# First block of a two-block network on one core: scores in two 128-row passes, value products in two rounded passes, gate projections ahead of the attention

## The chip, the cores and the metric

The kernel runs on one core of a Trainium2 chip. TensorE (PE) multiplies, with its weight loads shown as PEld; VectorE (DVE), ScalarE (ACT) and GpSimd (POOL) work on what it leaves; SyncE (SP) issues the transfers. The metric is the device time of one execution in microseconds (us), lower is better. The change is compared by the median of several runs.

## The reference, cut to what matters

The network has two blocks over 512 tokens of width 1024. The change touches the first block alone, a hybrid attention layer, everything in float32:

```python
qn = rope(rms_norm(heads(q_n)));  o_cmp, p = compressed_branch(qn, kc_cmp, vc_cmp)   # 31 compressed keys
o_sel = selected_branch(qn, ks, vs, sel_idx);  o_win = window_branch(qn, kw, vw)      # 512 keys, causal
o_nsa = (g0 * o_cmp + g1 * o_sel + g2 * o_win) * silu(z_n)
o_dsa = dsa_branch(qd, kd, vd, qi, ki, wi) * silu(z_d)       # each query keeps its 128 best keys
x = x + concat([o_nsa, o_dsa]) @ w_out
```

There are two groups (g) of four query heads (r) each, 64 channels a head, for each of two query sets (s = 0: the three branches of o_nsa, s = 1: o_dsa). The second block (two layers of feed-forward, mixing and feed-forward) follows and is not touched.

## The kernel before

Float32 accuracy is kept by splitting: `split` (L255 to L257) writes a rounded part hi with a copy on ACT and the remainder lo with a subtraction, on DVE by default. Rounded operands (F32R) take one pass of TensorE for each product, plain float32 ones are shown as two matmul records. `wload` (L259 to L264) loads 512 KB of weights and splits them (names raw, whi, wlo); `proj` (L501) is one projection of 128 columns: 24 matmuls of 512 columns into a bank "B", for the eight k-tiles of the input times the three products of hi and lo.

Block 1 is `block1` (L401). It emits, in this order: the projections 0 to 7 (indexer, compressed keys and values, keys) with the token-major values `tok` among them; the query projections 8 to 15, whose outputs are rotated (`rope`, L470) and stacked by `stack_q` and `stack_k` (L486 to L495); then the gate projections 16 and 17 (`post_z`, L783). `drain` (called at L833) then emits what is left of the background tasks, among them `topk` (L600), the choice of the 128 best keys: 16 rounds of MAX8 and MATCH_REPLACE8 on DVE for each of the query tiles 3, 2 and 1. Before that, `topk` is emitted at one round per 4.5 us of nominal product time.

The attention follows. Query tiles of 128 are taken in the order i = 3, 2, 1, 0, with keys up to n = 128 (i + 1). Each i has six steps (`step`, L839): for s = 0 two branches in each of two groups, for s = 1 one in each of two groups. A step makes four score tiles (one a head) in banks "A", takes them through a masked minimum on DVE (L852) and an exponential on ACT (L855), scales the rows by the reciprocal of their sum (DVE, ACT and POOL, L859 to L869), transposes each block of 128 keys (L878) into a bank "C", copies it to PT (L881 on ACT, L883 on DVE) and multiplies it with the values into a bank "D". A score takes two passes (`stacked`, L497): 128 rows hold the query's hi and lo against the key's hi twice, then 64 rows hold the query's hi against the key's lo. The value product is a plain float32 product with 64 output rows; both groups share one bank. `compressed` (L936) does the same for the compressed keys. `finish` (L925) multiplies the result by the gate z and splits it. The gate projections 18 to 23 are emitted one after each of the first six steps (`extra`, L1011; `more`, L1016), the first half of the output projections (`wout`, L989) after i = 2.

Emission order is a priority. A scheduler orders each engine's instructions: an instruction that is ready may go ahead of one emitted before it that is not. Memory is handed on tile by tile: a pool opened where another was closed waits for that one's last readers. The pool of the attention (PA) is opened where the projections' pool (PX) was.

Of the kernel before, what the change touches and what calls it, by code (L numbers as in the profile page):

```python
# [16 lines left out]
EPS = 1e-6  # L17
# [7 lines left out]
# ---------------------------------------------------------------- constants of the shapes  # L25
def _constants():
# [46 lines left out]
    # window over number of tokens in it, first and last eight tokens  # L73
# [10 lines left out]
    # rows p of the Fourier matrices; columns by residue of the frequency, 0 2 1 3 mod 4 and 0 1 mod 2  # L84
# [8 lines left out]
# ---------------------------------------------------------------- layout of the inputs  # L93
# [93 lines left out]
# columns of the packed per-partition vectors  # L187
# [13 lines left out]
class Tensor:  # L201
    """the tensor engine, with its newest product at hand"""
# [13 lines left out]
def build(tc, I, out, taps=None):  # L216
# [37 lines left out]
    # ------------------------------------------------------------ helpers  # L254
# [37 lines left out]
    def colsum(ps, sqs, nt):  # L292
        """ps[:, i] = sums over the partitions of the tiles in sqs, tokens on the partitions"""
# [5 lines left out]
    def rowcast(ps, cols, nt):  # L299
        """ps[p, t] = cols[t] on every partition"""  # L300
# [4 lines left out]
    # ------------------------------------------------------------ adaptive modulation  # L305
# [34 lines left out]
    def ada_done(l, c0, c1):  # L340
        """chunks c0..c1 of the nine become usable"""
# [13 lines left out]
    def wait(t):  # L355
        """the steps of a thread until t microseconds of products have been emitted"""
# [9 lines left out]
    def pace(t):  # L366
        """run a step of each background task per `every` microseconds of products"""
# [32 lines left out]
    # ------------------------------------------------------------ block 1  # L400
    def block1(fill, lh):  # L401
# [3 lines left out]
        XS = mkpool("xs", stack=b1)  # L405
        p1, pj = ExitStack(), ExitStack()
        P1 = mkpool("b1", stack=p1)
        PX = mkpool("pj", stack=pj)
# [8 lines left out]
        def bank(tag):  # L417
            return tl(PS, [128, 512], F32, tag, {"A": 3, "B": 2, "C": 2, "D": 1}[tag])
# [7 lines left out]
        def load_x():  # L426
# [5 lines left out]
            for k in range(KT):  # L432
                hi = tl(XS, [128, L], F32R, f"xhi{k}")
                lo = tl(XS, [128, L], F32R, f"xlo{k}")
# [30 lines left out]
            rb = tl(XS, [128, L], F32, "rb")  # L465
# [49 lines left out]
        # indexer queries and keys  # L515
# [17 lines left out]
        # token-major: values, gates, indexer weights  # L533
# [1486 lines left out]
```

## Time and profile before

| | |
|---|---|
| median of 3 runs | 3105.65 us |
| the runs | 3103.13, 3109.27, 3105.65 us |
| profiled execution | span 3109.3 us |
| PE, DVE, ACT, POOL busy share of the span | 97%, 57%, 44%, 33% |

The span agrees to the rounding with the highest of the three times, so nothing is seen to lie outside it. The PE share is an upper view: ends of matmuls are modelled, so the spacing of their starts says more than their durations. Views by stretch (busy time in each part of the span) tell which engine is full in which stage, the chain tells what the end waited for, and the groups give the duration of one instruction of a shape.

### The profile page before, as it was taken

The page shows a single profiled execution, that of the slowest core. Times are in us where ns is not written, and L with a number is a line of the kernel's source. Part 1 is how long each engine was busy: PE and PEld are TensorE (multiplying, and loading weights), DVE is VectorE, ACT ScalarE, POOL GpSimd, SP SyncE. Part 2 cuts the span into 40 slices and gives each one's busy share as a digit, 9 for nine tenths or more (in the row PEclk, how much of TensorE's full clock was granted, in tenths as well). Part 3 has the DMA queues.
Part 4 walks back from the last instruction along what each step waited for, and adds up shares of the span by engine and source line. Part 5 has one row for each costly group of instructions (what it writes and reads, how often), then busy time and mean ns, then how long its engine had stood idle before and what let it go on. Part 6 is the DMA issues. An engine that isn't in the chain of part 4 may idle for free.

```text
span 3109.3 us, 42513 instructions
## 1 busy us (share of the span) xinstructions
PE 3016.6 (97%) x16956; PEld 2521.5 (81%) x16956; DVE 1763.0 (57%) x3104; ACT 1363.7 (44%) x2410; POOL 1035.1 (33%) x556
## 2 busy tenths in 40 slices
PE   7799999999999999999999999999999999999998
PEld 6565467888888887678888888888888887698998
DVE  6996546764646536566667445443433457554545
ACT  6545546545535434445555344321322345442324
POOL 6763122667666222026896421000000142200001
PEclk9899899999999999999999999999999999999999
DMA  5311013333333311023444432121122221123223
GB/s 203 130 55 48 1 41 105 127 129 129 122 135 115 94 43 53 21 68 130 149 146 160 162 109 67 63 67 62 61 62 68 67 81 65 36 95 95 90 94 94
DMA packets 81720, 282.85 MB, mean 91 GB/s; under 512 B 9328, under 2 KB 13040, under 8 KB 80880
## 3 DMA queue, kind: packets, MB, share of 16 engines
q1 hardware_dynamic: 81520, 280.13, 27.3%
q8 instruction: 133, 2.18, 0.3%
q14 instruction: 67, 0.55, 0.1%
HBM read 277.99 MB, written 2.10 MB: 90 GB/s over the span
## 4 chain that ended last, share of the span: by engine, by line
PE 82%; DVE 9%; POOL 3%; ACT 3%; issue 2%; DMA 1%; SPq 0%; DVEq 0%; POOLq 0%; ACTq 0%
PE ps L209 72%; PE B L209 3%; PE A L209 3%; PE D L209 2%; POOL ajunk L332 2%; DVE wlo L257 1%; PE C L878 1%; POOL araw L332 1%; DMA araw<-in_ada_dram 1%; PE ps L1825 1%; DVE dm L606 1%; ACT whi L256 1%; DVE xll L1136 1%; DVE nt L1159 1%; DVE m L605 1%
## 5 line engine op out<-in xcount | busy, mean ns | idle before, releaser
L256 ACT ACTIVATE whi<-raw 128x1024 fp32r<-128x1024 f32 (+2 forms) x370 | 382.7, 1035 | 983.1 <-PE ps L209 764.4
L209 PE MATMUL ps<-xhl,whi 128*128 128x512 f32 (+2 forms) x1856 | 638.4, 352 | 3.1 <-ACT whi L256 1.6
L209 PE MATMUL ps<-xll,whi 128*128 128x512 f32 (+2 forms) x1856 | 635.9, 351 | 0.0
L209 PE MATMUL ps<-xhl,wlo 128*128 128x512 f32 (+2 forms) x1856 | 596.4, 351 | 6.3 <-DVE wlo L257 6.3
L257 DVE TENSOR_TENSOR wlo<-raw,whi 128x1024 fp32r<-128x1024 f32 (+2 forms) x342 | 501.3, 1467 | 127.5 <-ACT whi L256 120.3
L332 POOL TENSOR_TENSOR araw<-araw,cc 128x1024 f32<-128x1024 f32 x144 | 408.7, 2839 | 94.4 <-DMA araw<-in_ada_dram 80.0
L209 PEld LDWEIGHTS ps<-xhl,whi 128*128 128x128 f32 x1856 | 351.0, 189 | 51.3 <-ACT whi L256 2.0
L332 POOL TENSOR_TENSOR ajunk<-araw,cc 128x1024 f32<-128x1024 f32 x112 | 290.1, 2590 | 255.2 <-DMA araw<-in_ada_dram 234.9
L209 PEld LDWEIGHTS ps<-xll,whi 128*128 128x128 f32 x1856 | 352.3, 190 | 3.8
L209 PEld LDWEIGHTS ps<-xhl,wlo 128*128 128x128 f32 x1856 | 328.1, 190 | 11.4 <-DVE wlo L257 7.5
L209 PE MATMUL ps<-xlc,whi 128*128 128x258 f32 (+1 forms) x1112 | 315.6, 284 | 1.5 <-DVE xlc L1168 0.8
L209 PE MATMUL ps<-xhc,wlo 128*128 128x258 f32 (+1 forms) x1112 | 312.9, 282 | 0.0
L209 PE MATMUL ps<-xhc,whi 128*128 128x258 f32 (+1 forms) x1112 | 312.3, 282 | 0.4 <-ACT xhc L1167 0.4
L1096 POOL TENSOR_TENSOR accl<-accl,nt 128x512 f32<-128x512 f32 x24 | 33.4, 1390 | 800.1 <-ACT nt L1092 799.7
L209 PE MATMUL ps<-hll,whi 128*128 128x512 f32 (+1 forms) x752 | 284.8, 379 | 0.7 <-DVE hll L257 0.7
L209 PE MATMUL ps<-hhl,wlo 128*128 128x512 f32 (+1 forms) x752 | 285.3, 380 | 0.0
L209 PE MATMUL ps<-hhl,whi 128*128 128x512 f32 (+1 forms) x752 | 283.9, 379 | 0.0
L1271 DVE SCALAR_TENSOR_TENSOR hl<-ps,gtl,hl 128x512 f32<-128x512 f32 (+1 forms) x104 | 73.0, 709 | 350.7 <-PE ps L209 350.5
L209 PEld LDWEIGHTS ps<-xlc,whi 128*128 128x128 f32 x1112 | 209.4, 188 | 48.7 <-DVE xlc L1168 1.8
L209 PEld LDWEIGHTS ps<-xhc,whi 128*128 128x128 f32 x1112 | 208.8, 188 | 48.3 <-PE ps L209 1.7
L209 PEld LDWEIGHTS ps<-xhc,wlo 128*128 128x128 f32 x1112 | 210.5, 189 | 0.0
L1204 DVE SCALAR_TENSOR_TENSOR ps<-ps,rbl 128x512 f32<-128x512 f32 (+1 forms) x110 | 63.0, 590 | 236.6 <-PE ps L209 236.6
(578 smaller groups left out, 5905.4 us busy)
## 6 DMA issues: line engine op xcount, KB each, us to landing
raw<-in_w_dram SPq DMA_DIRECT2D x240, 512.0 KB, 3.5
araw<-in_ada_dram SPq DMA_DIRECT2D x144, 512.0 KB, 4.3
raw<-in_wo_dram SPq DMA_DIRECT2D x36, 512.0 KB, 3.4
raw<-in_wi_dram SPq DMA_DIRECT2D x34, 512.0 KB, 3.4
raw<-in_w_dram SPq DMA_DIRECT2D x36, 384.0 KB, 3.1
raw<-in_wg_dram SPq DMA_DIRECT2D x8, 512.0 KB, 3.5
cc<-in_cc_dram SPq DMA_DIRECT2D x3, 1024.0 KB, 5.0
sm<-in_sm_dram SPq DMA_DIRECT2D x2, 1282.0 KB, 7.1
```

What stands on the lines that cost most here:

```text
L209: self.newest = self.engine.matmul(*a, **k)
L256: S.activation(hi, x, AF.Copy)
L257: eng.tensor_tensor(out=lo, in0=x, in1=hi.bitcast(F32), op=ALU.subtract)
L332: m = G.tensor_tensor(out=o, in0=raw, in1=cc[:, v], op=ALU.mult)
L605: V.max(out=m8, in_=wk)
L606: V.match_replace(out=wk, in_to_replace=m8, in_values=wk, imm_value=-2e30)
L878: T.transpose(pt[:, 128 * r:128 * r + 128], Pm[:, r, 128 * kt:128 * kt + 128], ident)
L1096: (V if i == 7 else G).tensor_tensor(out=st.acc[:, c], in0=st.acc[:, c], in1=sq, op=ALU.add)
L1136: V.scalar_tensor_tensor(out=lo, in0=h, scalar=a, in1=hi.bitcast(F32), op0=ALU.mult, op1=ALU.subtract)
L1159: V.scalar_tensor_tensor(out=t, in0=st.h[k][:, c], scalar=st.A[:, k:k + 1], in1=st.rb[:, c], op0=ALU.mult, op1=ALU.mult)
L1204: V.scalar_tensor_tensor(out=pb, in0=pb, scalar=0.5, in1=rb, op0=ALU.mult, op1=ALU.mult)
L1271: V.scalar_tensor_tensor(out=st.h[m][:, c], in0=a, scalar=gates[st.name][:, m:m + 1], in1=st.h[m][:, c], op0=ALU.mult, op1=ALU.add)
```

## The change

Scores: the key's lo part is also written twice, so the second pass has 128 rows too. Values: hi and lo of the values lie beside each other as 128 stationary columns, the transposed probabilities are split into hi and lo, and two F32R passes replace the float32 product; each group has its own bank, and `gather` adds the two halves of it. All eight gate projections come before the attention, the input's second half is released then, and the forced emission of `topk` at that place is gone. Banks: A 3 to 2, D 1 to 2.

```diff
-            return tl(PS, [128, 512], F32, tag, {"A": 3, "B": 2, "C": 2, "D": 1}[tag])
+            return tl(PS, [128, 512], F32, tag, {"A": 2, "B": 2, "C": 2, "D": 2}[tag])
...
-                V.tensor_tensor(out=k[2][GS[g]], in0=y[GS[g]], in1=k[g][GS[g]].bitcast(F32), op=ALU.subtract)
+                V.tensor_tensor(out=k[2 + g][GS[g]], in0=y[GS[g]], in1=k[g][GS[g]].bitcast(F32), op=ALU.subtract)
                 S.activation(k[g][GS[1 - g]], y[GS[g]], AF.Copy)
+                S.activation(k[2 + g][GS[1 - g]], k[2 + g][GS[g]].bitcast(F32), AF.Copy)
...
             T.matmul(ps, q[g][:, qs], k[g][:, :n], start=True, stop=False)
-            T.matmul(ps, q[g][GS[g], qs], k[2][GS[g], :n], start=False, stop=True)
+            T.matmul(ps, q[g][:, qs], k[2 + g][:, :n], start=False, stop=True)
...
-                    S.activation(vt[i], pst[i][:, 0:384], AF.Copy, scale=rc[:, i:i + 1])
+                    pv_ = pst[i][:, 0:384].rearrange("p (b g d) -> p b g d", b=3, g=2)
+                    for g in range(2):
+                        hi, lo = vt[i][:, :, g, g], vt[i][:, :, g, 1 - g]
+                        S.activation(hi, pv_[:, :, g], AF.Copy, scale=rc[:, i:i + 1])
+                        V.scalar_tensor_tensor(out=lo, in0=pv_[:, :, g], scalar=rc[:, i:i + 1], in1=hi.bitcast(F32),
+                                               op0=ALU.mult, op1=ALU.subtract)
...
-        proj(16, post_z(0, 0))
-        proj(17, post_z(0, 1))
+        flush()
+        for b in list(bg):
+            if b[0] is fill:
+                for _ in fill:
+                    pass
+                bg.remove(b)
+        aes.close()
+        PZ = mkpool("pz", stack=p1, side="right")
+        zz.extend(tl(PZ, [128, 4, L], F32, f"z{n_}") for n_ in range(2))
+        for n_ in range(2):
+            for r in range(4):
+                proj(16 + 4 * n_ + r, post_z(n_, r), G if r % 2 else V)
         flush()
         while threads:
             advance()
         pj.close()
-
-        # attention
+        xe.close()
         at = ExitStack()
-        drain()
-        aes.close()
         PA = mkpool("at", stack=at)
-        zz.append(tl(PA, [128, 4, L], F32, "z1"))
...
-                    PT = PTs[kt] = tl(PA, [128, L], F32, "PT", 3)
-                    if kt % 2 == 0 or i == 3:
-                        S.activation(PT, pt, AF.Copy)
-                    else:
-                        V.tensor_copy(PT, pt)
+                    PTs[kt] = [tl(PA, [128, L], F32R, f"PT{p}", 3) for p in "hl"]
+                    split(*PTs[kt], pt)
...
-                        state["acc"] = bank("D")
-                    acc = state["acc"]
-                    T.matmul(acc[gs, :], vt[kt][:, vcol + 64 * g:vcol + 64 * g + 64], PTs[kt],
-                             start=gcol is None and kt == 0, stop=last and kt == i)
-                    if fin and kt == i:
-                        finish(acc, i, s)
+                        state["acc", g] = bank("D")
+                    acc = state["acc", g]
+                    v = vt[kt][:, br, g].rearrange("p a d -> p (a d)")
+                    for n_, P_ in enumerate(PTs[kt]):
+                        T.matmul(acc, v, P_, start=first and kt == n_ == 0, stop=last and kt == i and n_ == 1)
+                    if last and kt == i:
+                        gather(acc, i, s, g)
...
+        def gather(acc, i, s, g):
+            if g == 0:
+                state["o"] = tl(PA, [128, 4, 128], F32, "o", 2)
+            o = state["o"]
+            og = o[GS[g]].rearrange("p r q -> p (r q)")
+            S.activation(og, acc[GS[1 - g]], AF.Copy)
+            V.tensor_tensor(out=og, in0=acc[GS[g]], in1=og, op=ALU.add)
+            if g == 0:
+                return
...
-            V.scalar_tensor_tensor(out=o, in0=acc.rearrange("p (r q) -> p r q", r=4), scalar=0.5,
-                                   in1=zz[s][:, :, sl], op0=ALU.mult, op1=ALU.mult)
+            V.tensor_tensor(out=o, in0=o, in1=zz[s][:, :, sl], op=ALU.mult)
...
-        extra = [lambda r=r: proj(16 + r, post_z(0, r), G) for r in (2, 3)]
-        extra += [lambda r=r: proj(20 + r, post_z(1, r), G) for r in range(4)]
+        extra = []
```

The compressed branch gets the same split of its probabilities and values; `post_z` folds the factor 0.5 in.

## Rows read from the trace of the kernel before

**Rows 1.** Busy time by stretch: each engine's us (instructions), granted clock, DMA.
```profile
130.00:245.00 115.00, 97.68 (x422) 76.12 (x420) 111.52 (x228) 55.22 (x81) 72.00 (x43) 0.90 0.20 69
...
245.00:489.00 244.00, 241.24 (x962) 137.39 (x962) 124.23 (x377) 122.40 (x310) 52.57 (x33) 0.92 0.11 35
```

**Rows 2.** The chain that ended last, 245 to 489 us, shares by line.
```profile
by line: PE A L209 28.8%; PE D L209 28.5%; PE B L209 24.6%; PE C L878 15.0%; PE C L970 1.7%; DVE o L929 0.6%; ACT PT L881 0.2%; ACT xhi L256 0.2%; DVE dm L606 0.2%; DVE P L852 0.1%; issue 0.1%; DVE Pc L947 0.1%; DVE den L859 0.0%; DVE mx L8
```

**Rows 3.** DVE in order of time (start, us): first score and last gating.
```profile
245.38 0.73 DVE L852 CUSTOM_DVE_ANT_0 P<-A,blk1c,rq0y 128x512 f32<-128x512 f32 x1
...
488.16 0.69 DVE L929 SCALAR_TENSOR_TENSOR o<-D,z 128x512 f32<-128x512 f32 x1 [4.26 <-PE D L209]
```

**Rows 4.** PE in order of time, 276 to 289 us (start, us, xcount).
```profile
276.82 0.40 PE L209 MATMUL B<-xhi,whi 128*128 128x512 f32 x1
277.05 0.39 PE L209 MATMUL B<-xlo,whi 128*128 128x512 f32 x1
...
283.33 2.60 PE L209 MATMUL A<-k,q 128*128 128x512 f32 x6
285.86 0.50 PE L209 MATMUL B<-xhi,whi 128*128 128x512 f32 x1
...
287.69 1.07 PE L209 MATMUL D<-PT,v 128*64 128x512 f32 x2
288.70 0.66 PE L878 MATMUL C<-cst,P 128*128 128x128 f32 x4
```

**Rows 5.** PE groups by shape, 245 to 489 us: xcount, busy, mean ns, idle before.
```profile
L209 PE MATMUL D<-PT,v 128*64 128x512 f32 x120 | 67.5, 650 | 1.5 <-DVE den L859 0.9 <-ACT PT L881 0.6
L878 PE MATMUL C<-cst,P 128*128 128x128 f32 x240 | 42.0, 299 | 0.0
...
L209 PE MATMUL B<-xhi,wlo 128*128 128x512 f32 x34 | 14.4, 424 | 0.0
```

**Rows 6.** DVE groups by shape, 245 to 489 us.
```profile
L883 DVE COPY PT<-C 128x512 f32<-128x512 f32 x12 | 8.3, 690 | 13.9 <-PE C L878 12.1 <-PE D L209 1.7
...
L789 DVE SCALAR_TENSOR_TENSOR z<-zt,z 128x512 f32<-128x512 f32 x6 | 7.8, 1304 | 2.1 <-ACT zt L788 2.1
...
L859 DVE RECIPROCAL den<-den 128x4 f32<-128x4 f32 x24 | 4.2, 174 | 10.2 <-ACT P L855 10.2
L786 DVE TENSOR_TENSOR z<-B,rb 128x512 f32<-128x512 f32 x6 | 4.1, 687 | 7.3 <-PE B L209 7.3
```

**Rows 7.** ACT groups by shape, 245 to 489 us.
```profile
L881 ACT ACTIVATE PT<-C 128x512 f32<-128x512 f32 x48 | 28.4, 595 | 59.0 <-PE C L878 58.8
...
L256 ACT ACTIVATE whi<-raw 128x1024 fp32r<-128x1024 f32 x13 | 13.7, 1051 | 13.5 <-PE B L209 7.3 <-issue 6.2
...
L788 ACT ACTIVATE zt<-z 128x512 f32<-128x512 f32 x6 | 3.7, 621 | 0.0
```

**Rows 8.** The choice of keys on DVE: groups, 120 to 250 us.
```profile
L605 DVE MAX8 m<-dm 128x8 f32<-128x384 f32 x16 | 8.8, 552 | 0.2
L606 DVE MATCH_REPLACE8 dm<-m,dm 128x384 f32<-128x384 f32 x16 | 8.7, 542 | 0.1
...
L605 DVE MAX8 m<-dm 128x8 f32<-128x256 f32 x16 | 6.8, 423 | 0.2
L606 DVE MATCH_REPLACE8 dm<-m,dm 128x256 f32<-128x256 f32 x16 | 6.5, 409 | 0.1
```

**Rows 9.** The same in order of time: its first round and its last operation.
```profile
123.92 0.69 DVE L605 MAX8 m<-dm 128x8 f32<-128x512 f32 x1
...
246.04 0.28 DVE L608 TENSOR_SCALAR dm<-dm 128x256 f32<-128x256 f32 x1
```

**Rows 10.** Busy time by stretch where PE has gaps; columns as in rows 1.
```profile
130.00:140.00 10.00, 4.57 (x26) 3.71 (x24) 10.00 (x16) 5.44 (x9) 5.96 (x3) 0.84 0.49 171
140.00:150.00 10.00, 6.25 (x29) 5.79 (x30) 8.95 (x14) 2.30 (x4) 6.72 (x4) 0.65 0.39 148
150.00:160.00 10.00, 10.00 (x47) 7.42 (x45) 9.04 (x17) 3.14 (x5) 9.33 (x6) 1.00 0.16 53
```

More of the change, by code (lines that the diff above doesn't have):

```diff
@@ L432, in load_x @@
             for k in range(KT):
-                hi = tl(XS, [128, L], F32R, f"xhi{k}")
-                lo = tl(XS, [128, L], F32R, f"xlo{k}")
+                hi, lo = (tl(XA if k < 4 else XB, [128, L], F32R, f"x{p}{k}") for p in ("hi", "lo"))
                 g = vec[:, V_NG + k:V_NG + k + 1]
@@ L531, in post_ki @@
             rope(y, ki)
-        vt = [tl(P1, [128, 384], F32, f"v{i}") for i in range(4)]
+        vt = [tl(P1, [128, 3, 2, 2, 64], F32R, f"v{i}") for i in range(4)]
         gate = tl(P1, [128, 4, 24], F32, "gate")
@@ L609, in topk, with qtile @@
                 chosen[0] = i
-        kT = [[tl(P1, [128, L], F32R, f"k{n}{a}") for a in range(3)] for n in range(3)]
-        qT = [[tl(P1, [128, L], F32R, f"q{n}{a}") for a in range(2)] for n in range(8)]
-        kcT = [tl(P1, [128, 32], F32R, f"kc{n}") for n in range(3)]
-        vc = tl(P1, [31, 2, 64], F32, "vc")
+        kT = [[tl(P1, [128, L], F32R, f"k{n}{a}") for a in range(4)] for n in range(3)]
+        qT = [None] * 8
+        def qtile(n, a, dt=F32R):
+            return tl(P1, [128, L], dt, f"q{n}{a}")
+        kcT = [tl(P1, [128, 32], F32R, f"kc{n}") for n in range(4)]
+        vc = tl(P1, [31, 2, 2, 64], F32R, "vc")
         parts = {}
@@ L631, in post @@
                                     op=ALU.add)
-                    hi, lo = (q[:, 0:496] for q in qT[4 + 2 * ci + half])
+                    hi, lo = (qtile(4 + 2 * ci + half, n_)[:, 0:496] for n_ in range(2))
                     split(hi, lo, a.rearrange("p g c r -> p (g c r)"))
@@ L684, in ctail @@
                                  cw2[:, 256 + 64 * m:320 + 64 * m], start=m == 0, stop=m == 1)
-                V.tensor_copy(vc.rearrange("p g d -> p (g d)"), po[0:31, 0:128])
+                for g in range(2):
+                    split(vc[:, g, g], vc[:, g, 1 - g], po[0:31, 64 * g:64 * g + 64])
                 return
@@ L713, in block1 @@
         kms = tl(PX, [128, 3, 4, 2], F32, "kms")
-        zz = [tl(P1, [128, 4, L], F32, "z0")]
-        ky = [zz[0][:, n] for n in range(3)]
+        ky = [qtile(2 + n // 2, n % 2, F32) for n in range(3)]
         def post_k(n_, gcol):
@@ L830, in block1, with step @@
         pj.close()
+        xe.close()
         at = ExitStack()
-        drain()
-        aes.close()
         PA = mkpool("at", stack=at)
-        zz.append(tl(PA, [128, 4, L], F32, "z1"))
         state = {}
-        def step(i, g, s, kTt, mask, vcol, gcol, first, last, fin, ahead=[], behind=[]):
+        def step(i, g, s, kTt, mask, br, gcol, first, last, fin, ahead=[], behind=[]):
             n = 128 * (i + 1)
-            gs = slice(64 * g, 64 * g + 64)
             q4, rq4 = qT[4 * s:4 * s + 4], rq[s]
@@ L977, in f @@
                 def f():
-                    if g == 0:
-                        state["acc"] = bank("D")
-                    T.matmul(state["acc"][64 * g:64 * g + 64, :], vc[:, g], PTs[g], start=True, stop=False)
+                    acc = state["acc", g] = bank("D")
+                    v = vc[:, g].rearrange("p a d -> p (a d)")
+                    for n_, P_ in enumerate(PTs[g]):
+                        T.matmul(acc, v, P_, start=n_ == 0, stop=False)
                 return f
@@ L1022, in block1 @@
             if i % 2:
-                pool, th, tlo = (PA, "ohi", "olo") if i == 3 else (XS, "xhi", "xlo")
-                state["oh", i // 2] = [(tl(pool, [128, 2, 256], F32R, f"{th}{a}"),
-                                        tl(pool, [128, 2, 256], F32R, f"{tlo}{a}")) for a in range(4)]
+                pool, tag = (PA, "o") if i == 3 else (XA, "x")
+                state["oh", i // 2] = [[tl(pool, [128, 2, 256], F32R, f"{tag}{p}{a}") for p in ("hi", "lo")]
+                                       for a in range(4)]
             n = 128 * (i + 1)
@@ L1033, in block1 @@
                 more(i)
[L1034 removed]
+                step(i, g, 0, kT[1], mask, 1, 2, False, True, g == 1)
                 more(i)
```

33 lines of the change are left out of this document (16 added, 17 removed).

## The prediction, made before the changed kernel was run

> **What bounds the kernel now.** I read the view by stretch first, since the share over the whole span (PE 97%) mixes stages. In the last stretch ahead of the attention, 130 to 245 us, DVE is busy 111.5 of 115 us and PE 97.7 [rows 1]: the choice of keys, the rotations and the splits fill DVE, and PE waits for it now and then. From 245 to 489 us, the attention, it is the other way round: PE 241.2 of 244 us, DVE 124.2, ACT 122.4 [rows 1]. The chain of the same stretch agrees: 98% of it is PE, and by banks the scores (A) take 28.8%, the value products (D) 28.5%, the gate projections and output projections (B) 24.6%, the transposes (C) 15% [rows 2]. The attention runs from its first score on DVE at 245.4 to the end of the last gating at 488.9 us: 243.5 us [rows 3]. So the change works on the engine that binds here, and the question is what binds once PE is relieved.
>
> **The change part by part.** Only starts tell what a matmul costs, so prices are spacings.
>
> Scores. Dense projections of 512 columns start 0.23 us apart. A run of six score matmuls, 128 rows and 64 rows in turn, takes from 283.33 to 285.86 us, 0.42 each [rows 4]. The 24 steps have 4 heads and 2 passes, 192 such matmuls. If two passes of 128 rows go at the dense spacing, each saves 0.19 us; I take the same for the narrower tiles, and nothing for the compressed branch: 192 x 0.19 = 36 us of PE. The bounds are 0 (the spacing has another cause) and about 40. The Trainium skill says in "TensorE: Matmul & The Clock Gate", section "Why this matters for your kernels", that a single product with few rows takes the same time as one with 128. By that rule this part would save nothing on PE. The six score matmuls speak against it [rows 4], though they don't say whether the row count or the alternation costs the 0.19; it is a rival below.
>
> Value products. One is two records and takes 287.69 to 288.70 us, 1.0 us [rows 4]; there are 60 of them (120 records, [rows 5]) and 8 in the compressed branch. Two F32R passes at 0.23 take 0.46: 68 x 0.54 = 37 us of PE saved.
>
> Gates. 100 matmuls of gate projections lie behind 245 us (34 in the group shown and 33 in each of the two others, [rows 5]). There they fill time in which PE would wait for the softmax. Moved ahead they cost 100 x 0.23 = 23 us, and the attention's tiles lie in memory that the projections' temporaries and part of the input held, so its first softmax waits for the last gate's evacuation too: 0.69 + 0.62 + 1.30 = 2.6 us [rows 6, 7]. The attention starts 25.6 us later. Nothing hides this: that stage had PE busy 85%, but its gaps come from waits on DVE that the gates, being emitted last, meet only at the end. From below, one projection (5.5 us) and the 2.6 us may be hidden: 17.5; from above 28. The move also changes which engine splits two of the gates' weights (POOL to DVE) and where their eight 512 KB loads stand in SP's queue: each has the 5.5 us of a projection, and DMA is 20% busy there [rows 1].
>
> PE's sum in the attention is then 241 - 23 - 36 - 37 = 145 us.
>
> DVE. It loses the six gates' evacuations (4.1 + 7.8 us) and 12 copies to PT (8.3 us) [rows 6]. It gains the lo part of every transposed block, 68 subtractions out of PSUM; the nearest row is the copy out of PSUM of the same size, 0.69 us [rows 6]: 47 us. It gains 16 half additions in gather at the same price, 11 us. 124.2 - 11.9 - 8.3 + 47 + 11 = 162 us.
>
> ACT. It loses six weight copies (6.3) and six tanh (3.7), and gains 12 copies to PT and 16 in gather at about 0.6 [rows 7]: 122.4 - 10 + 17 = 129 us.
>
> So DVE becomes the bound of the attention, with ACT close behind, and each now waits for the other twice a step: DVE for the exponential's sums, ACT for the scores, and new, DVE's subtraction for ACT's hi copy. The 162 us can't be reached. DVE waited 10.2 us for the exponentials ahead of the reciprocals [rows 6], and that stays: 172 is the lower end. The upper end adds one whole hi copy, 0.595 us [rows 7], to each of the 68 subtractions: 172 + 40 = 212. Neither row is nearer (DVE always has other heads' scores to take, but only two banks A now, and its order is fixed), so I take the middle, 192 us. Two banks A instead of three lie within these ends: a score waits until DVE has taken the one two before it, and behind it on PE wait the transposes that ACT needs.
>
> Choice of keys. Emitted at one round per 4.5 us, eight queries, one compressed unit and eight gates (8 x 5.1 + 1.3 + 8 x 5.1 = 83 us) bring 18 of 48 rounds ahead of the attention, and the forced rest is gone. But before, only 11 rounds were emitted ahead of the forced ones, and yet the rounds ran steadily from 123.9 to 246 us [rows 9], beside the query projections. A ready round is taken forward whenever DVE is free in the plan, so I expect them there again and cost the move at nothing; the cover is the 25 us by which the stage grows. If it is gone, 30 rounds, 14 x (0.55 + 0.54) + 16 x (0.42 + 0.41) = 29 us of DVE [rows 8], land in the attention.
>
> Values and keys. The values' evacuation has four more copies on ACT, some 2 us at most, 0 at least: 1 us taken. The keys' extra eight copies on ACT lie beside a DVE that is fuller (ACT 55 of 115 us, [rows 1]): nothing. The second block is the same.
>
> Sum against the profiled execution: 3109.3 + 25.6 - (243.5 - 192) + 1 = 3084.4 us. The median lies 3.65 below the profiled execution: 3080.8, so 3081 us. With 172 and 17.5 it is 3053, with 212 and 28 3103.
>
> **The rivals.**
>
> Rival 1, PE still binds or DVE loses nothing to waits. For it: PE fills 99% of the stage today [rows 1], and the order is planned with all waits known. Attention 162 us, start 17.5 later: 3043 us. Against it: the lo parts wait for ACT by construction.
>
> Rival 2, the choice of keys moves into the attention. DVE has 162 + 29 there, with 10 to 50 us of waits 201 to 241, middle 221; the stage before gets back up to half of PE's 17 us of gaps [rows 1], 8 us: 3105.65 + 25.6 - 8 - 22.5 + 1 = 3102 us, no change that can be told.
>
> Rival 3, on the other side: the granted clock falls. With the gates gone PE has 145 us of work in 192, 75% busy. Where PE had gaps, 46% and 63% busy at 130 to 150 us, the clock was 0.84 and 0.65, and back at 1.00 in the next 10 us with PE full [rows 10]; in the attention it is 0.92 [rows 1], so the 145 us are 133 at full speed. If a share x of the work ran at 1.2 GHz, PE would need 133 (1 + x). It passes DVE's 192 at x = 0.44 and makes the kernel slower beyond 218 us, x = 0.64. At x = 0.8 it is 240: 3105.65 + 25.6 - 3.5 + 1 = 3129 us. Against it: even 130 to 150 us had only half at the low level. The Trainium skill ("TensorE: Matmul & The Clock Gate", section "PE-mode transpose") says that transposes don't count as activity for the clock as products do; the attention keeps its 240 transposes [rows 5] and loses products, so by that rule this rival gains. No row here separates the two.
>
> Rival 4, the change doesn't do what it says: two 128-row passes also start 0.42 apart. PE has 145 + 36 = 181 us, still under 192 but no longer hidden: some 205 us, 3094 us.
>
> **How the numbers follow.** Forecast 0.56 (3053 to 3103), rival 1 0.11 (3043), rival 2 0.13 (3102), rival 3 0.14 (3129), rival 4 0.06 (3094). About 0.2% (6 us) is what can be told from no change. Faster: nearly all of the forecast (0.51), rivals 1 and 4 (0.16), a little of rival 2: 0.70. Same: 0.14. Slower: 0.16. The range leaves out most of rival 1 below and rival 3 above: 3050 to 3110 us.
>
> **What would show it.** By stretch, the attention's first score near 271 us, DVE the fullest engine behind it, PE near 75%. Score matmuls 0.23 apart, value products 0.46. DVE's subtractions out of PSUM 0.69 us each, idle ahead of them put down to ACT's hi copy. MAX8 over by about 270 us. The prediction is wrong if the score spacing stays 0.42, if MAX8 is seen among the scores, if the clock in the attention falls under 0.7, or if the attention starts before 260 or takes over 215 us.

## The result, and the profile after

The changed kernel takes 3068.9 us (3064.84 to 3069.45), the kernel before beside it 3105.8 us: a ratio of 0.9878, 95% interval 0.986 to 0.9895. It is 1.2% faster. The prediction said 3081 us, with a range from 3050 to 3110: the direction and the range held, and the gain is 12 us larger than forecast. The profiled execution has a span of 3067.5 us, 41.8 us less than that of before, though the medians lie only 36.9 us apart: a span is some 1.8 us shorter than its execution's time (3067.5 against 3069.37 here), so the 3109.3 us profiled before belong, by that estimate, to an execution of some 3111 us, slower than the three runs listed with it; that the span met the highest of them was chance.

Busy time by stretch, the kernel after (columns as in [rows 1]: stretch, length, then PE, PEld, DVE, ACT and POOL in us, granted clock, DMA):

```profile
130.00:245.00 115.00, 100.57 (x424) 77.46 (x424) 109.69 (x235) 57.52 (x89) 70.56 (x42) 0.88 0.21 69
245.00:275.00 30.00, 24.53 (x108) 19.85 (x109) 19.04 (x23) 9.82 (x12) 9.52 (x4) 0.96 0.28 90
275.00:447.00 172.00, 155.31 (x864) 119.23 (x863) 153.96 (x433) 128.72 (x328) 42.19 (x28) 0.93 0.10 34
447.00:3067.00 2620.00, 2572.01 (x15108) 2223.50 (x15108) 1438.47 (x2389) 1105.84 (x1884) 818.07 (x440) 0.99 0.29 93
```

The stretch 130 to 245 us is nearly what it was. A new one follows, 30 us of gate projections. The attention has shrunk, and taken as a whole no engine fills it: PE 155, DVE 154 and ACT 129 of 172 us, where PE had 241 of 244 [rows 1]. That is a mean over four query tiles with different limits; the tiles i = 3, 2, 1 and 0 end near 335, 375, 422 and 447 us:

```profile
275.00:335.00 60.00, 54.49 (x255) 35.98 (x254) 56.68 (x141) 46.54 (x108) 12.02 (x7) 0.94 0.02 8
335.00:375.00 40.00, 36.53 (x205) 26.80 (x205) 37.43 (x110) 32.08 (x83) 8.52 (x6) 1.00 0.01 1
375.00:422.00 47.00, 44.29 (x322) 39.17 (x320) 42.34 (x116) 34.26 (x86) 19.85 (x12) 1.00 0.28 91
422.00:447.00 25.00, 20.00 (x86) 17.28 (x85) 17.51 (x70) 15.83 (x53) 1.81 (x3) 0.65 0.13 42
```

DVE is busy 94% of the first two, PE 94% of the third, which also holds output projections, and no engine fills the last, where the granted clock is 0.65.

The edges of the attention, DVE in order of time (start, us, then the instruction, in brackets the idle time ahead of it):

```profile
271.48 2.41 DVE L802 SCALAR_TENSOR_TENSOR z<-t,z 128x512 f32<-128x512 f32 x1 [0.73 <-ACT t L801]
273.81 0.47 DVE L972 TENSOR_TENSOR Pc<-A,blk1c 128x124 f32<-128x124 f32 x2
...
275.47 0.75 DVE L872 CUSTOM_DVE_ANT_0 P<-A,blk1c,rq0y 128x512 f32<-128x512 f32 x1 [0.29 <-PE A L209]
...
445.77 0.69 DVE L955 TENSOR_TENSOR o<-o,z 128x512 f32<-128x512 f32 x1
```

From the first score at 275.47 to the end of the last gating at 446.46 it is 171.0 us, against 243.5 [rows 3]. In the terms of the prediction's sum:

| us | forecast | measured |
| --- | --- | --- |
| first score later (gates, values) | +25.6 +1 | +30.1 |
| attention | -51.5 | -72.5 |
| what lies behind it (2620.4 before, 2621.0 after) | 0 | +0.6 |
| sum | -24.9 | -41.8 |

The chain that ended last, 275 to 447 us, shares by line:

```profile
by line: DVE P L872 12.0%; DVE PTl L257 11.9%; PE A L209 10.9%; PE D L209 8.8%; DVE P L887 6.3%; issue 6.2%; PE B L209 5.9%; PE C L898 5.7%; ACT P L875 5.5%; ACT PTh L256 4.3%; DVE o L950 3.5%; DVE o L955 2.0%; POOL wlo L257 1.4%; DVE Pc L9
```

Before, 98% of this chain was PE [rows 2]. Now it passes from engine to engine, with the scores' masking on DVE and the new subtractions ahead of any line of PE. The spacings of PE, in order of time (start, us, xcount):

```profile
300.67 1.09 PE L209 MATMUL A<-k,q 128*128 128x512 f32 x4
...
312.13 0.71 PE L209 MATMUL A<-k,q 128*128 128x512 f32 x2
312.68 0.40 PE L209 MATMUL D<-PTh,v 128*128 128x512 f32 x1
312.91 0.39 PE L209 MATMUL D<-PTl,v 128*128 128x512 f32 x1
...
313.81 1.33 PE L209 MATMUL A<-k,q 128*128 128x512 f32 x4
315.08 0.50 PE L209 MATMUL D<-PTh,v 128*128 128x512 f32 x1
315.42 0.43 PE L209 MATMUL D<-PTl,v 128*128 128x512 f32 x1
```

Four score passes take 1.09 us. With the last one's own 0.40 off, three steps take 0.69: 0.23 each, where it was 0.42 [rows 4]. Two passes of a value product start 0.23 apart at one place (312.68, 312.91) and 0.34 apart at another (315.08, 315.42). Both pairs stand behind scores; what differs is the load of the pass's weights (PEld):

```profile
312.45 0.19 PEld L209 LDWEIGHTS D<-PTh,v 128*128 128x128 f32 x1
...
315.08 0.19 PEld L209 LDWEIGHTS D<-PTh,v 128*128 128x128 f32 x1 [0.36 <-ACT PTh L256]
```

The first load ran 0.23 us ahead of its pass. The second began with its pass, since it waited for ACT's copy. Of 110 value passes at full clock 34 had their load 0.1 us or more ahead and are followed 0.23 later (median). For 45 it began with the pass, and the next start is 0.34 later where PE did not wait again. The other 31, most of them right behind transposes, have 0.32. Over the attention the median is 0.32 to 0.33: a value product costs 0.65, not 0.46.

DVE's new work in the same stretch, groups by shape (xcount, busy us, mean ns, idle before and its releasers):

```profile
L257 DVE TENSOR_TENSOR PTl<-C,PTh 128x512 fp32r<-128x512 f32 x60 | 40.7, 683 | 4.2 <-ACT PTh L256 3.8
...
L950 DVE TENSOR_TENSOR o<-D,o 64x512 f32<-64x512 f32 x16 | 11.0, 685 | 4.5 <-ACT o L949 4.2
...
L879 DVE RECIPROCAL den<-den 128x4 f32<-128x4 f32 x24 | 4.1, 171 | 2.2 <-ACT P L875 2.1
```

The prices are those of the copy out of PSUM, 0.69 us [rows 6]. But the waits are small: 3.8 us for ACT's hi copies and 2.1 for the exponentials, which had been 10.2 [rows 6].

### The profile page after: what moved, and what is told of

It is laid out like the page before. It is cut to its first block, busy times and chain, and to the rows that moved or that the text cites. A ratio compares the mean times of both kernels' runs of the same rounds, so it can differ in the third digit from the quotient of the medians.

```text
span 3067.5 us, 42647 instructions
## 1 busy us (share of the span) xinstructions
PE 2954.9 (96%) x16956; PEld 2518.5 (82%) x16956; DVE 1821.2 (59%) x3187; ACT 1383.8 (45%) x2452; POOL 1030.5 (34%) x554
## 4 chain that ended last, share of the span: by engine, by line
PE 76%; DVE 13%; ACT 4%; POOL 3%; issue 2%; DMA 2%; SPq 0%; DVEq 0%; POOLq 0%; ACTq 0%
PE ps L209 71%; PE B L209 2%; DVE wlo L257 2%; POOL ajunk L332 2%; DMA araw<-in_ada_dram 1%; POOL araw L332 1%; ACT whi L256 1%; PE ps L1848 1%; PE A L209 1%; DVE dm L612 1%; DVE P L872 1%; DVE PTl L257 1%; PE D L209 1%; DVE xll L1159 1%; DVE m L611 1%
```

## The experiments

My theory was that each of the three parts acts by the engine that binds at that moment: the gates ahead are a shift of 23 to 30 us that gives nothing by itself, the narrower PE work gives what PE loses until DVE binds, and the split's subtractions on DVE then set the length. The rivals are in the expectations. Times are medians, each beside runs of the kernel before on the same chip. "Attention" is from the first score on DVE to the end of the last gating.

### The three parts one by one

**The gate projections alone, put into the kernel before.**

```diff
-        proj(16, post_z(0, 0))
-        proj(17, post_z(0, 1))
+        flush()
...
+        PZ = mkpool("pz", stack=p1, side="right")
+        zz.append(tl(PZ, [128, 4, L], F32, "z1"))
+        for n_ in range(2):
+            for r in range(4):
+                proj(16 + 4 * n_ + r, post_z(n_, r), G if r % 2 else V)
...
-        extra = [lambda r=r: proj(16 + r, post_z(0, r), G) for r in (2, 3)]
-        extra += [lambda r=r: proj(20 + r, post_z(1, r), G) for r in range(4)]
+        extra = []
```

> The kernel before with only the gate projections moved ahead of the attention. Theory: in the attention TensorE binds, so what leaves it comes off its length nearly in full: first score 30 us later (275 us, as in the changed kernel), attention 243.5 - 23 = 220 us, in all some 6 us slower, 3112 us. Rival: the gates only filled waits of TensorE and were free there; then the attention stays near 243 us and the kernel is 30 us slower, 3136 us.

Measured: 3111.71 us against 3110.97, ratio 1.0005 (0.9994 to 1.0016): no change. In the profile the end of the attention comes 3.3 us earlier, at 485.5 us, but its execution is the fastest of ten (3106.27 us), so that is no gain either. The chain, 275 to 432 us, shows why: PE still has all of it.

```profile
by line: PE A L209 34.9%; PE D L209 34.4%; PE C L886 20.2%; PE B L209 8.4%; PE C L978 1.4%; ACT PT L889 0.8%; issue 0.1%
```

PE is full where the gates now stand (30.00 of 30 us, 245 to 275) and where they stood, so what it does first is paid now or later. One part went otherwise than I had put it: DVE took a first score at 241.6 us, in the middle of the gates, and the second step began at 272.7. Why a score could start so early here was not separated. The first score is no clean edge of the attention in this kernel, so its end is what I compare.

**Scores and gates, with the float32 value products of before.** The changed kernel with these lines back (and what they need for `vt`, `vc` and `gather`):

```diff
-                    PTs[kt] = [tl(PA, [128, L], F32R, f"PT{p}", 3) for p in "hl"]
-                    split(*PTs[kt], pt)
+                    PT = PTs[kt] = tl(PA, [128, L], F32, "PT", 3)
+                    if kt % 2 == 0 or i == 3:
+                        S.activation(PT, pt, AF.Copy)
+                    else:
+                        V.tensor_copy(PT, pt)
...
-                    for n_, P_ in enumerate(PTs[kt]):
-                        T.matmul(acc, v, P_, start=first and kt == n_ == 0, stop=last and kt == i and n_ == 1)
+                    T.matmul(acc[GS[g], :], vt[kt][:, 128 * br + 64 * g:128 * br + 64 * g + 64], PTs[kt],
+                             start=gcol is None and kt == 0, stop=last and kt == i)
```

> The changed kernel with the value products back in plain float32 (one bank for both groups, no lo part of the probabilities), so gates ahead and 128-row scores remain. Theory: the score passes lose 36 us of TensorE, which binds again without the value part: attention 220 - 36 = 184 us, 3105.65 + 30 - 59.5 = 3076 us; score matmuls 0.23 us apart. Rival (row count without a price): scores stay 0.42 us apart, attention 220 us, 3112 us.

Measured: 3081.3 us, ratio 0.9902 (0.9887 to 0.9917), attention 189.1 us from 272.5 to 461.5.

```profile
272.00:462.00 190.00, 185.04 (x864) 107.36 (x862) 110.63 (x360) 113.94 (x300) 40.85 (x28) 0.92 0.09 31
```

PE has 185 of 190 us, DVE 111: PE binds again, as the theory had it, 5 us longer than expected.

**Rounded values and gates, with a second score pass of 64 rows.**

```diff
-            T.matmul(ps, q[g][:, qs], k[2 + g][:, :n], start=False, stop=True)
+            T.matmul(ps, q[g][GS[g], qs], k[2 + g][GS[g], :n], start=False, stop=True)
```

> The changed kernel with 64 rows in the second score pass, so gates ahead and rounded value products remain. Theory: TensorE gets 36 us back and is about level with VectorE: attention 185 to 195 us against 171, 3083 to 3093 us. Rival (VectorE alone binds the changed attention): 171 us as in the changed kernel, 3069 us.

Measured: 3100.39 us, ratio 0.9968 (0.9955 to 0.998), attention 203.0 us. Both expectations were too short. Stretches of 25 us:

```profile
275.00:300.00 25.00, 23.32 (x56) 12.14 (x57) 16.52 (x40) 11.38 (x25) 4.11 (x3) 0.59 0.06 22
...
450.00:475.00 25.00, 24.99 (x80) 17.19 (x80) 18.42 (x78) 17.04 (x59) 2.41 (x4) 0.60 0.19 63
```

PE is nearly full, and in two of these stretches the granted clock is 0.59 and 0.60, mostly the lower of its two levels. Over this attention it is 0.837, in the changed kernel 0.929. PE's busy time is 198.0 us against 154.8. At the clock 0.929 the 198.0 would be 198.0 x 0.837 / 0.929 = 178.4. So of the 43 us, by this estimate from means, some 24 are spacing and some 20 the clock. The starts price the spacing higher, at 192 x 0.19 and 48 x 0.1, together 41 us: short waits that the modelled ends hide count as busy in the changed kernel, so the split is rough. I had expected the spacing alone.

With the gates ahead in all four, the ends of the attention make a square: neither part 485.5, scores alone 461.5, values alone 480.4, both 446.5. The scores bring 24 us alone and 34 beside the rounded values. The values bring 5 alone and 15 beside the scores. The scores alone without the gates ahead, and both parts with the gates left inside, were not tried.

### Row count or alternation

In `a_rows64` four score passes of 128 and 64 rows in turn took 1.69 us, 0.42 apart as before; in the changed kernel they are 0.23 apart. What is dear, 64 rows or the change? This kernel makes every pass of 64 rows, three of them to a score, so that no score pass differs from the one ahead of it:

```diff
-            T.matmul(ps, q[g][:, qs], k[g][:, :n], start=True, stop=False)
-            T.matmul(ps, q[g][:, qs], k[2 + g][:, :n], start=False, stop=True)
+            T.matmul(ps, q[g][GS[g], qs], k[g][GS[g], :n], start=True, stop=False)
+            T.matmul(ps, q[g][GS[g], qs], k[2 + g][GS[g], :n], start=False, stop=False)
+            T.matmul(ps, q[g][GS[g], qs], k[2 + g][GS[g], :n], start=False, stop=True)
```

> The changed kernel with three score passes that all have 64 rows (query hi by key hi, query hi by key lo, and the second once more where the product of query lo would stand, which is left out of the result). What is read is the spacing of starts inside a run of score matmuls of 512 columns. Theory (the change between 128 and 64 rows costs, not the row count): 0.23 us inside such a run, and some 0.2 more only where rows change, at its ends. Rival (a pass of 64 rows is slow by itself): 0.42 us throughout.

Measured, one run: 3118.73 us against 3107.22. A group of score passes of the mixed kernel (`a_rows64`), then one of this kernel, both at full clock:

```profile
300.52 1.69 PE L209 MATMUL A<-k,q 128*128 128x512 f32 x4
```

```profile
303.44 1.66 PE L209 MATMUL A<-k,q 64*128 64x512 f32 x6
```

Six passes of 64 rows in 1.66 us, less the last one's 0.45: 0.24 apart. So 64 rows cost no more and no less than 128; the change between them costs 0.18 to 0.19 us a pass. The compressed scores, 32 columns, tell the same: medians of 0.112 with 64 rows throughout, 0.112 with 128, 0.21 mixed. The Trainium skill says in "TensorEngine Tiling (Array Packing)", section "Key Properties", that changing the tiling mode drains TensorE; the trace, which writes these tiles as `64*128` and `128*128`, agrees with 0.42 against 0.24. That a few rows take as long as 128, which rival 4 rested on, is true here too; what rival 4 lacked was the change.

The total of this kernel, which ran once, is longer, 217.0 us of attention. It has a third pass, and its clock is lower:

```profile
325.00:350.00 25.00, 25.00 (x75) 16.18 (x76) 14.07 (x37) 10.69 (x26) 3.32 (x2) 0.56 0.00 0
```

### What the subtractions cost

**Without them.** Both value passes use the hi part, so the number of PE's passes stays and DVE loses the lo parts of the whole-block probabilities; the kernel leaves out the correction by lo:

```diff
-                    PTs[kt] = [tl(PA, [128, L], F32R, f"PT{p}", 3) for p in "hl"]
-                    split(*PTs[kt], pt)
+                    PTs[kt] = [tl(PA, [128, L], F32R, "PTh", 3)] * 2
+                    S.activation(PTs[kt][0], pt, AF.Copy)
```

> The changed kernel without the 60 subtractions that make the lo part of the transposed probabilities; the second value pass is run with the hi part again, so TensorE and ScalarE have the same work (the correction by lo is left out of the result). Theory: VectorE binds the changed attention, and 60 x 0.68 = 41 us less work there shortens it until ScalarE (129 us) and TensorE (155 us busy) bind: 171 to about 150 us, 3048 us. Rival: the chain of a step (score, exponential, scaling, transposes) sets the pace: no more than 5 us, 3064 us or more.

Measured: 3056.29 us, ratio 0.982 (0.9806 to 0.9835), attention 158.3 us.

```profile
275.00:329.00 54.00, 51.65 (x260) 36.67 (x259) 42.17 (x117) 46.17 (x108) 12.12 (x7) 0.93 0.03 10
329.00:364.00 35.00, 32.47 (x205) 26.52 (x203) 28.36 (x91) 30.74 (x81) 7.59 (x6) 1.00 0.00 1
364.00:411.00 47.00, 43.55 (x317) 38.80 (x317) 35.16 (x104) 34.17 (x88) 19.93 (x12) 1.00 0.26 89
```

DVE loses 33.9 us of work, the attention 12.7. These stretches are its first three query tiles. The first two, where DVE had been full, are 6 and 5 us shorter; the third, where PE was the fuller, is as long as before, though DVE lost 7 us there too. So the subtractions set the length where DVE is full, and in the first tile only until PE is (51.65 of 54 us). The test is not wholly clean: PE's busy time falls as well, from 154.8 to 145.3 us, since a second pass that reads the hi part needn't wait for a subtraction and is followed 0.23 us later instead of 0.33 (medians). The chain from 275 to 432 us:

```profile
by line: PE A L209 14.2%; PE D L209 13.6%; PE C L898 11.4%; PE B L209 10.7%; DVE P L872 10.1%; ACT P L875 8.3%; ACT PTh L900 4.3%; issue 3.9%; DVE P L887 3.7%; DVE o L950 3.3%; DVE o L955 1.6%; PE C L995 1.4%; DVE xlo L257 1.4%; DVE cm__779
```

Over the whole attention PE's four banks, the masking of scores on DVE and the exponentials on ACT share it.

**Without them and without the second value pass**:

```diff
-                    PTs[kt] = [tl(PA, [128, L], F32R, f"PT{p}", 3) for p in "hl"]
-                    split(*PTs[kt], pt)
+                    PTs[kt] = [tl(PA, [128, L], F32R, "PTh", 3)]
+                    S.activation(PTs[kt][0], pt, AF.Copy)
...
-                        T.matmul(acc, v, P_, start=first and kt == n_ == 0, stop=last and kt == i and n_ == 1)
+                        T.matmul(acc, v, P_, start=first and kt == n_ == 0, stop=last and kt == i and n_ == 0)
```

> The changed kernel with one value pass instead of two and without the subtractions for it (the lo part of the probabilities is left out of the result; the compressed branch is unchanged). VectorE loses the same 34 us as in the run without the subtractions, TensorE 14 us more. Theory (with VectorE relieved, TensorE and ScalarE bind): attention 158 - 10 = 148 us, 3046 us. Rival (the chain of a step binds by then): 156 to 158 us, 3054 us or more.

Measured: 3054.38 us, ratio 0.9828 (0.9812 to 0.9844), attention 154.6 us.

```profile
277.00:432.00 155.00, 138.19 (x802) 108.83 (x801) 120.32 (x371) 125.49 (x328) 41.66 (x28) 0.91 0.11 36
```

PE has 7 us less than without the subtractions alone, the attention is 3.7 us shorter, and by their medians the two kernels can't be told apart. That is the rival's side: PE 138, DVE 120 and ACT 125 of 155 us, none full, and in no query tile has PE more than 91%. What is left may be the way of one step through all three engines (scores, masking, exponential, scaling, transposes, copy, value products); that is argued, no run shows it.

**The second head's scaling on POOL** takes work off DVE without touching the order of a step:

```diff
-                        elif r_ < 3 or fin and i == 0:
+                        elif r_ < 1 or fin and i == 0:
```

> The changed kernel with the scaling of the second head of each step on GpSimd instead of VectorE. Theory: VectorE (154 of 171 us busy) binds the attention, 12 us less on it gain 5 to 10 us, 3059 to 3064 us. Rival: the scaling lies in the chain of a step and takes 1.76 us on GpSimd against 0.69, twice in a row for the last two heads: no gain or up to 10 us slower, 3069 to 3079 us.

Measured: 3072.91 us, ratio 0.9884 (0.9865 to 0.9903), attention 172.2 us: DVE's busy time fell by 10.5 us and the time didn't follow. The rival was right.

```profile
270.00:443.00 173.00, 153.66 (x864) 119.83 (x863) 143.71 (x411) 127.54 (x326) 68.83 (x50) 0.93 0.10 34
```

This run doesn't acquit DVE. A scaling of 512 columns takes 1.71 us on POOL here (mean), 0.69 on DVE, and it lies in the chain of a step: the first query tile became 2 us shorter, the second 3 us longer. The three together: work taken off DVE pays in the two tiles that DVE fills, but not where something slower takes its place in the step.

### Two banks for the scores

The prediction counted the cut from three banks A to two among the waits. Here every second score of the query tiles 3 and 2 goes to a bank B:

```diff
-                    ps = bank("A")
+                    ps = bank("B" if i > 1 and r % 2 else "A")
```

> The changed kernel with every second score tile of the query tiles 3 and 2 in a bank B, which no projection uses there, so four score banks instead of two. Theory: TensorE has slack in the attention and VectorE's order is fixed, two banks cost little: within 5 us of 3069. Rival (the cut from three banks to two holds the scores back): 8 us or more faster, below 3061 us.

Measured: 3079.36 us, ratio 0.9904 (0.9889 to 0.9919), attention 180.4 us, 9 longer than in the changed kernel. Neither expectation has that. What PE waited for in this kernel, 274 to 455 us (us in total, times, longest):

```profile
...
PE A L209 <- DVE mx L872: 3.4, 6, 0.9
PE C L995 <- DVE Pc L986: 2.9, 1, 2.9
PE A L209 <- DVE Pc L972: 2.7, 1, 2.7
```

The waits for DVE's scores, which the extra banks were to relieve, are 3.4 us; in the changed kernel they are 2.3 us. (The weight loads, which wait ahead of the passes, have 9.0 us of it here and 10.0 in the changed kernel.) So there was little to relieve. What came in are two waits on the compressed probabilities, 5.6 us, and a lower clock, 0.889. The order of the work came out otherwise, and whether the shared bank B, the order or the clock made the 9 us stays open.

### The choice of keys inside the attention

The prediction's rival 2, made true: each round of `topk` ordered behind the newest matmul.

```diff
-                    V.max(out=m8, in_=wk)
+                    mx_ = V.max(out=m8, in_=wk)
+                    tc.add_manual_dep(mx_.ins, T.newest.ins.name, ORDER)
```

> The changed kernel with every round of the choice of keys ordered behind the newest matmul at its place of emission, so that the later rounds run in the attention. Theory: VectorE binds there, 29 us more of it lengthen the attention by 20 to 30 us, and the stage before gets back 0 to 8 us: 3085 to 3098 us. Rival (VectorE has slack in the attention): within 6 us of 3069.

Measured: 3073.59 us, ratio 0.9882 (0.9868 to 0.9897). The stage ahead and the attention by stretch, the attention's first three query tiles, then DVE's groups of rounds in the attention:

```profile
130.00:245.00 115.00, 111.25 (x498) 87.75 (x499) 94.17 (x153) 64.45 (x97) 76.24 (x44) 0.95 0.25 83
258.00:448.00 190.00, 168.39 (x862) 126.69 (x860) 173.49 (x523) 129.96 (x326) 41.27 (x28) 0.88 0.09 30
```

```profile
258.00:328.00 70.00, 61.62 (x255) 39.68 (x253) 66.03 (x177) 47.45 (x108) 11.10 (x7) 0.88 0.01 4
328.00:374.00 46.00, 40.04 (x207) 29.52 (x207) 44.17 (x137) 32.95 (x83) 8.42 (x6) 0.93 0.00 1
374.00:425.00 51.00, 48.64 (x321) 41.90 (x321) 47.22 (x150) 35.74 (x90) 20.53 (x13) 0.93 0.26 84
```

```profile
L611 DVE MAX8 m<-dm 128x8 f32<-128x384 f32 x14 | 7.6, 544 | 0.0
...
L611 DVE MAX8 m<-dm 128x8 f32<-128x256 f32 x16 | 6.6, 415 | 0.1
```

Thirty of the 48 rounds lie in the attention, the number of the prediction's price, and it grew by 19.4 us (190.4). In the three tiles DVE has 9, 7 and 5 us more to do than in the changed kernel, and they are 10, 6 and 4 us longer: what is added to DVE there is paid nearly in full. But the stage ahead gave back 17.4 us: the first score comes at 258.0, PE has 111 of 115 us busy there and DVE 94, where it was 101 and 110. I had put the give-back at 8 us or less. DVE held PE up in that stage nearly one for one, so the place of the rounds hardly matters.

### The start of the attention

**The first tiles in the gates' memory.** The compressed probabilities `Pc` and `cm_` and the gates' tanh tile go into the pool of the gates, so that the attention's first step need not wait for the projections' temporaries:

```diff
-                th = tmp()
+                th = tl(zp[0], [128, L], F32, "zt")
...
-            Pc = tl(PA, [128, 8, 31], F32, "Pc", 2)
+            Pc = tl(PZ, [128, 8, 31], F32, "Pc", 2)
...
-                    m_ = tl(PA, [128, 8], F32, "cm_", 2)
+                    m_ = tl(PZ, [128, 8], F32, "cm_", 2)
```

> The changed kernel with the compressed branch's probabilities and the gates' tanh in the pool of the gates, so that the attention's first tiles no longer lie on memory that the last gate still reads. Theory: the late start (275.5 us against 271 us for the last gate product) is that memory; the first scores start between 255 and 268 us beside the last gate products and the kernel gains 5 to 12 us, 3057 to 3064 us. Rival: TensorE is full with gate products until 271 us and the order puts the scores behind them anyway: first score at 272 us or later, 3066 us or more.

Measured: 3065.52 us, ratio 0.9863 (0.9847 to 0.988), attention from 272.2, 172.5 long. The start gains 3.3 us, the attention loses 1.5: the rival's side, and the interval overlaps that of the changed kernel.

**The same with 16 small scalings of the queries' norms moved from DVE to ACT:**

```diff
+            rcm = tl(P1, [128, 4], F32, "rcm")
+            V.tensor_scalar(rcm, rc, -0.125, None, op0=ALU.mult)
...
-                    V.tensor_scalar(ms[n_][:, i], ms[n_][:, i], rc2[:, i:i + 1], None, op0=ALU.mult)
+                    S.activation(ms[n_][:, i], ms[n_][:, i], AF.Copy, scale=rc2[:, i:i + 1])
...
-                    V.tensor_scalar(r4[:, i], r4[:, i], rc[:, i:i + 1], -0.125, op0=ALU.mult, op1=ALU.mult)
+                    S.activation(r4[:, i], r4[:, i], AF.Copy, scale=st_["rcm"][:, i:i + 1])
```

> The run with the attention's first tiles off the gates' memory, and with the sixteen small scalings of the query norms (128 by 8, 0.63 and 0.69 us each on VectorE while GpSimd works, though 0.16 us for a copy of that size out of PSUM) on ScalarE, which is half idle there. Theory: VectorE binds the stage ahead of the attention (110 of 115 us), 10 us less on it brings the first score 4 to 8 us earlier, 3058 to 3062 us. Rival: TensorE's gate products bind there: first score at 272 us as before, 3065 us.

Measured: 3059.59 us, ratio 0.9846 (0.9832 to 0.9861); first score at 269.5, attention 170.5. The total is as expected, its parts are not: the first score is 2.7 us earlier than in `a_early`, where 4 to 8 were expected, and the attention 2.0 us shorter. That work taken off DVE pays in the stage ahead, where PE waits for DVE, fits the earlier score, but the interval overlaps that of `a_early`. This is the fastest of the kernels that keep the whole computation; its interval and that of the changed kernel (0.986 to 0.9895) just touch.

## Why the prediction was right, and where it was off

**What bound the attention, and the direction: right.** PE bound, and cutting PE's work moved the end. Both other parts of the change showed it: with float32 value products PE binds again at 185 of 190 us.

**Scores: right, with one term missed.** The dense passes came to 0.23 as forecast, and `a_all64` settles that it is the alternation. Taken at nothing were the compressed scores; by the medians of their starts they went from 0.21 to 0.112, 48 x 0.1 = 5 us. The narrower tiles, for which I took the 0.19 of the wide ones, saved it at 256 columns (0.31 to 0.12) but some 0.11 at 384 and at 128, by medians that hold short waits.

**Value products: right in kind, too cheap.** 0.65 instead of 0.46, 68 x 0.19 = 13 us more of PE. The price of a dense run, in which each load of weights goes ahead, was used for passes that start as soon as their operand is ready (0.34) or right behind transposes (0.32), which the row [rows 4] showed and I did not weigh. `a_nosub` bears this out: its second pass, with the hi part long written, is back at 0.23. PE came out at 154.8 us, 10 above the forecast 145.

**DVE's sum: 162 forecast, 153.7 measured.** The term that failed is a mean duration used as a time slot. In order of time, a subtraction of the changed kernel and what follows it:

```profile
300.87 0.68 DVE L257 TENSOR_TENSOR PTl<-C,PTh 128x512 fp32r<-128x512 f32 x1
301.47 0.67 DVE L950 TENSOR_TENSOR o<-D,o 64x512 f32<-64x512 f32 x1
```

It lasts 0.68 and its follower starts 0.60 behind it. Up to the next start, the 68 subtractions occupy 42 us, not 47. For PE the prediction used spacings, for DVE it did not. That is 5 of the 8 us; the rest was not separated.

**DVE's waits: the step that failed most.** Forecast were 10 + 0 to 40, taken 30; measured 171.0 - 153.7 = 17.3. The 10.2 us for the exponentials were taken as staying. They fell to 2.1, presumably since DVE has more work to do meanwhile. Of the 0 to 40 for ACT's hi copies 3.8 came. The middle of a wide interval was taken for want of a row, though one thing pointed low: with four heads in flight DVE nearly always had another head's score ready. The two terms together, 8 + 13 = 21 us, are the whole miss in the attention (192 against 171).

**"DVE becomes the bound": right for the first two of the four query tiles, 100 of 171 us.** DVE is busy 94% there, what `a_late` added to it lengthened them nearly one for one, and what `a_nosub` took off shortened these two and hardly the others. In the third tile PE is the fuller again, and in the last none is, at a clock of 0.65. The prediction laid one engine's work and waits over the whole attention. By tile DVE's idle time is 3.0, 2.5, 4.7 and 7.0 us: most of what was forecast as its waits stands where something else sets the length.

**The start: 26.6 forecast, 30.1 measured.** The choice of keys starts 2.9 us later (126.81, [rows 9] had 123.92), where 1 was taken for the values; which of the operations ahead of it make the 2.9 was not separated:

```profile
126.81 0.69 DVE L611 MAX8 m<-dm 128x8 f32<-128x512 f32 x1
...
245.83 0.41 DVE L611 MAX8 m<-dm 128x8 f32<-128x256 f32 x1
```

And the last gate's evacuation took 2.41 us, where the mean of 1.30 [rows 6] was used; 1.9 + 1.1 of the 3.5 us are thereby named. The bounds above, 28 and 2, just fail to hold it. The cover for the choice of keys held: its last MAX8 is over at 246.2 us, ahead of the attention.

**The rivals.** Rival 1 (3043 us) had DVE without waits and 162 us of attention; the attention lies nearer to that (171) than to my 192, but the late start took 12.6 us of it back: that the total came so near the forecast is in part two errors of opposite sign. Rival 2 did not happen, and where it was made to happen it cost 5 us or less (the intervals overlap), not 21, its step "the stage before gets back 8 us" being wrong. Rival 3 did not happen over the changed attention as a whole, 0.929 against 0.923, though in its last tile the clock is 0.65, where before it was 0.94 (458 to 489 us). It is no idle fear, as the kernels with 64-row passes show. Rival 4 fell with the spacing.

## What to carry to other kernels

Price an operation by the distance to the next start on its engine, among the neighbours that it will really have: both mis-sized prices of this case were a mean duration, or a spacing from another neighbourhood. Moving work ahead of a full engine is a zero sum; it pays only when the same change makes that engine stop being full. And read who is full tile by tile: over the whole attention no engine passed 91%, yet two tiles were DVE's and one PE's, and work taken off DVE paid in its own two.

## What the runs showed of the hardware

**A change of row count on PE costs time, the count itself doesn't.** The loads of the weights show where the time goes, first in the kernel before, with 128 and 64 rows in turn, then in the changed one:

```profile
284.16 0.19 PEld L209 LDWEIGHTS A<-k,q 128*128 128x128 f32 x1 [0.24 <-issue]
284.58 0.18 PEld L209 LDWEIGHTS A<-k,q 64*128 64x128 f32 x1 [0.24 <-issue]
```

```profile
300.44 0.89 PEld L209 LDWEIGHTS A<-k,q 128*128 128x128 f32 x4
```

Where the rows change, a load begins 0.24 us after the end of the one ahead, so 0.42 apart, like the passes. Where they don't, four loads take 0.89, and the first begins 0.23 ahead of its pass (300.67). The 0.18 to 0.19 that a change costs is as long as a load. A compressed value product of the changed kernel, with 31 rows among 128-row scores, shows it too; it is followed 0.43 later:

```profile
330.85 0.50 PE L209 MATMUL D<-PTh,vc 31*128 31x512 f32 x1
331.28 0.62 PE L209 MATMUL A<-k,q 128*128 128x384 f32 x2
```

**The clock can fall while PE is full.** The prediction tied a lower clock to gaps of PE [rows 10]. The kernel before already had a full stretch at a low clock:

```profile
370.00:380.00 10.00, 10.00 (x27) 5.32 (x27) 3.58 (x12) 3.43 (x9) 1.28 (x1) 0.66 0.00 1
```

In `a_all64`, run once, a stretch with PE busy 25.00 of 25 us was granted 0.56, and both kernels with 64-row passes came to 0.81 and 0.84 over the attention. The changed kernel, with PE busy 90%, had 0.93. What it is in those passes that goes with the lower clock stays open.

**POOL can hold up DVE.** A gating of the changed kernel on DVE with POOL idle, and the split on POOL that ran beside the last one (271.48, 2.41 us, in the fence on the attention's edges):

```profile
247.94 0.69 DVE L802 SCALAR_TENSOR_TENSOR z<-t,z 128x512 f32<-128x512 f32 x1 [0.18 <-ACT t L801]
```

```profile
271.00 2.34 POOL L257 TENSOR_TENSOR wlo<-raw,whi 128x1024 fp32r<-128x1024 f32 x1 [3.15 <-ACT whi L256]
```

The split ends at 273.34, the last gating 0.55 us later, near its undisturbed 0.69: it seems to have waited for POOL and then run. The three other gatings that met a split end 0.55 to 0.56 us behind it too. The Trainium skill ("SBUF — State Buffer", section "SBUF: two separate sides") calls the ports that DVE and GpSimd share an exclusive lock, held for the whole instruction, when the DVE operation has two inputs in SBUF and the GpSimd one reads SBUF; 2.41 against 0.69 us agrees. Here it stood on the way to the first score, 1.1 us longer than the mean that the forecast had used.
